# Turning the order of wide and narrow matmuls from chunk to chunk in the weight-stationary projections

## The chip, the cores and the metric

The kernel runs on one core of a Trainium2 chip; the other cores are idle. The metric is the device time of one execution in microseconds (us), the median of a few runs. The engines of the core are named as in the profile: PE is TensorE (its matmuls), PEld its weight loads, DVE is VectorE, ACT is ScalarE, POOL is GpSimd and SP is SyncE, whose queue issues the DMAs.

## The reference

A small decoder trunk of two layers over 256 positions and 1024 channels, in float32. Every sub-layer is applied as a post-norm with a scaled residual. The gated feed-forward network (FFN) stands twice in each layer and has an inner width of 2816:

```python
def swiglu(x, w_gate, w_up, w_down):
    return (jax.nn.silu(x @ w_gate) * (x @ w_up)) @ w_down

for l in range(DEPTH):                                   # DEPTH = 2
    x = layer_norm(alpha * x + 0.5 * swiglu(x, gate[l, 0], up[l, 0], down[l, 0]), ...)
    mem_kv = mem @ w_kv_mem[l]                           # 256 memory tokens
    u = x @ w_in_conv[0]  or  x @ w_in_mlstm[0]          # layer 0, layer 1
    tok = short_conv_mixer(u[...])  or  mlstm_mixer(u[...])
    xa = memory_cross_attention(u[..., -256:], mem_kv)
    x = layer_norm(alpha * x + concat([tok, xa]) @ w_out[l], ...)
    x = layer_norm(alpha * x + 0.5 * swiglu(x, gate[l, 1], up[l, 1], down[l, 1]), ...)
```

The output is the last x, 256 by 1024.

## The kernel before

Float32 matmuls are made of float32r products. Each operand is split into a high part, rounded to float32r, and a low part, the rest. The product of two operands is then high times high, high times low and low times high. Weights arrive by DMA on the SP queue in pieces of 128 x 2048 (`raw`). `split` (lines 98 to 100) turns each piece into a high tile `wh` (a copy on ACT, line 99) and a low tile `wl` (a subtraction on DVE, line 100), mostly in halves of 1024 columns. Five pieces can be held split at a time and three raw ones. The order of the pieces is a list written out at the start; the next piece is loaded and split when an earlier one is taken with `get`.

Activations are kept transposed in tiles of `[128, 8, 2, 256]`: eight chunks `k` of 128 channels, and in each the high and the low part of 256 positions side by side, 512 columns in all.

There are two ways of multiplying:

- **`mm3` (lines 171 to 177)**: the activation is the stationary operand, the weights stream past it. For each chunk it issues three matmuls, 512 columns wide mostly. The down projection of the FFN (`y`), the output projection (`yo`) and the first groups of the later FFNs (`gx`) are made like this.
- **`mmw` (lines 179 to 182)**: the weights are the stationary operand ("weight-stationary"). For each chunk it issues a pair: a wide matmul with `wh` that streams all 512 columns (high and low positions), and a narrow one with `wl` that streams the 256 columns of the high part into the first half of the same PSUM bank. Eight chunks are summed in one bank; then `comb` (lines 184 to 187) adds the two halves, on ACT (line 186) and DVE (line 187). Each matmul here has a weight load of its own, 128 x 128.

`mmw` is called from `gu_ws` (lines 271 to 303), the gate and up projection of one group of 256 inner channels: four banks of eight chunks each, 32 pairs; from `mem_kv` (line 388, tiles `kb`); and from `proj_ws` (line 407), which serves the cross-attention's query (`xq`), the gates and the input of the convolution (`cg`, `cx`, `cb`) and the query and key of the mLSTM (`qkp`).

An FFN runs over 11 groups `g`. A steady step is one `gu_ws` (32 pairs) and one `down` of the group before (24 matmuls of `mm3`, 512 wide). In the first FFN all groups go through `gu_ws`, and for `g` below 2 the loop over chunks is the outer one and the four banks the inner one; in the three other FFNs the groups 0 and 1 go through `gu_xs` (tiles `gx`) and the remaining nine through `gu_ws`.

The program is written in the Tile framework, which finds the waits between engines itself and may put instructions of an engine in another order than the source where it expects an operand later than another. So in group 2 of the first FFN some wide matmuls stand ahead of their narrow ones.

Of the kernel before, what the change touches and what calls it, by code (L numbers as in the profile page):

```python
# [14 lines left out]
P = 128  # L15
T = 256
D = 1024
KC = D // P
# [13 lines left out]
def trunk(ctx: ExitStack, tc: tile.TileContext, d, out):  # L32
    nc = tc.nc
    pe, act, dve, pool = nc.tensor, nc.scalar, nc.vector, nc.gpsimd
# [16 lines left out]
    def mbank(name):  # L51
        return psm.tile([P, 512], F32, tag="mm", name=name)

    def tmp(name):
        return tp.tile([P, 512], F32, tag="t", name=name)
# [79 lines left out]
    def get(*key):  # L135
        while state["next"] < len(pieces) and state["next"] <= state["used"] + 1:
            trace_piece()
        assert pieces[state["used"]][0] == key, (pieces[state["used"]][0], key)
        state["used"] += 1
        return made.pop(key)  # L140
# [11 lines left out]
    for k in range(KC):  # L152
# [3 lines left out]
        s = slice((k % 4) * 512, (k % 4) * 512 + 512)  # L156
# [3 lines left out]
    cur = {"x": x0}  # L160
# [10 lines left out]
    def mm3(o, a, b, start, stop):  # L171

        ah, al = a
        bh, bl = b
        pe.matmul(o, ah, bh, start=start, stop=False)  # L175
        pe.matmul(o, ah, bl, start=False, stop=False)  # L176
        pe.matmul(o, al, bh, start=False, stop=stop)  # L177

    def mmw(bank, w, a, start, stop):

        pe.matmul(bank, w[0], a.rearrange("p c t -> p (c t)"), start=start, stop=False)  # L181
        pe.matmul(bank[:, :T], w[1], a[:, 0], start=False, stop=stop)  # L182

    def comb(o, bank):

        act.activation(o, bank[:, T:], AF.Copy)  # L186
        dve.tensor_add(o, o, bank[:, :T])  # L187
# [4 lines left out]
    def xpart(k, t):  # L192
        return cur["x"][:, k, 0, tsl(t)], cur["x"][:, k, 1, tsl(t)]
# [70 lines left out]
    def ffn(l, j, xs_groups, i, last=False):  # L264
        hT = {}
        y = {}

        def new_h(g):
            hT[g] = hp.tile([P, 2, 2, T], F32R, tag="h", name=f"h{l}{j}_{g}")

        def gu_ws(g, outer=False):
            w = [get("gu", l, j, g, 0), get("gu", l, j, g, 1)]
            new_h(g)
            banks = {}

            def mm(fc, m, k):
                if k == 0:
                    bank = ybank if outer and g == 0 else mbank
                    banks[fc, m] = bank(f"gu{l}{j}_{g}_{fc}{m}")
                c0 = (k % 4) * 512 + m * 256 + fc * P  # L280
                wk = w[k // 4]
                mmw(banks[fc, m], (wk[0][:, c0:c0 + P], wk[1][:, c0:c0 + P]), cur["x"][:, k],
                    k == 0, k == KC - 1)

            if outer:
                for k in range(KC):
                    for fc in range(2):
                        for m in range(2):
                            mm(fc, m, k)
            for fc in range(2):  # L290
                t_ = tmp(f"s{l}{j}_{g}_{fc}")
                for m in range(2):
                    if not outer:
                        for k in range(KC):
                            mm(fc, m, k)
                    comb(t_[:, m * 256:(m + 1) * 256], banks[fc, m])
                    if m == 0:
                        act.activation(t_[:, :256], t_[:, :256], AF.Silu)  # L298
                dve.scalar_tensor_tensor(t_[:, 256:], t_[:, :256], 0.5, t_[:, 256:],  # L299
                                         op0=ALU.mult, op1=ALU.mult)  # L300
                hh = hT[g][:, 0, fc, :]
                act.activation(hh, t_[:, 256:], AF.Copy)  # L302
                dve.tensor_sub(hT[g][:, 1, fc, :], t_[:, 256:], hh.bitcast(F32))  # L303

        xsw = {}

        def gu_xs(g, t, mid=None):
            if t == 0:
                xsw[g] = [get("gu", l, j, g, 0), get("gu", l, j, g, 1)]
                new_h(g)  # L310
            w = xsw[g]
            b = mbank(f"gx{l}{j}_{g}_{t}")
            for k in range(KC):
                wk = w[k // 4]
                s = slice((k % 4) * 512, (k % 4) * 512 + 512)
                mm3(b, xpart(k, t), (wk[0][:, s], wk[1][:, s]), k == 0, k == KC - 1)
                if k == 5 and mid:
                    mid()
            t_ = tmp(f"sx{l}{j}_{g}_{t}")
            act.activation(t_[:, :256], b[:, :256], AF.Silu)  # L320
            dve.scalar_tensor_tensor(t_[:, 256:], t_[:, :256], 0.5, b[:, 256:],
                                     op0=ALU.mult, op1=ALU.mult)

            def rest():
                hx(g, t, t_)
            return rest

        def hx(g, t, t_):
            tb = mbank(f"hx{l}{j}_{g}_{t}")
            for fc in range(2):  # L330
                pe.transpose(tb[:, fc * P:(fc + 1) * P], t_[:, 256 + fc * P:256 + (fc + 1) * P], ident)
            tv = tb[:, :256].rearrange("p (c t) -> p c t", c=2)
            hh = hT[g][:, 0, :, tsl(t)]
            act.activation(hh, tv, AF.Copy)
            dve.tensor_sub(hT[g][:, 1, :, tsl(t)], tv, hh.bitcast(F32))

        def down(g, t, hs, w):
            for fc in range(2):
                a = (hT[g][:, 0, fc, tsl(t)], hT[g][:, 1, fc, tsl(t)])
                for h in hs:  # L340
                    if (t, h) not in y:
                        y[t, h] = ybank(f"y{l}{j}_{t}{h}")
                    s = slice(fc * D + 512 * h, fc * D + 512 * h + 512)
                    mm3(y[t, h], a, (w[0][:, s], w[1][:, s]), g == 0 and fc == 0,
                        g == NG - 1 and fc == 1)

        late = []
        for t in range(2):
            for g in range(xs_groups):
                late.append(gu_xs(g, t, pending if (t, g) == (0, xs_groups - 1) else None))  # L350
                if len(late) > 1:
                    late.pop(0)()
        for g in range(NG):
            if g == 2:
                if i == 0:
                    late_loads()
                gb = load_ln(i)
            if g >= xs_groups:
                gu_ws(g, outer=(l, j) == (0, 0) and g < 2)
                while late:  # L360
                    late.pop(0)()
            for q in downs_after(g, xs_groups):
                w = get("wd", l, j, q)
                for t in range(2):
                    down(q, t, (0, 1), w)
        nx = None if last else new_act(f"x{i}")
        ws = {g: get("wd", l, j, g) for g in range(NG - TAIL, NG)}

        def tail(t):
            for h in range(2):  # L370
                for g in range(NG - TAIL, NG):
                    down(g, t, (h,), ws[g])
                ln_half(i, t, h, y[t, h])
        norm_both(i, gb, nx, tail)
# [4 lines left out]
    def mem_kv(mem):  # L379
        w = [get("kv", q) for q in range(4)]  # L380
        for l in range(2):
            kvs[l] = (consts.tile([P, 2, T], F32, name=f"kT{l}"), consts.tile([P, 2, T], F32, name=f"vm{l}"))
        for c in range(4):
            b = mbank(f"kb{c}")
            for k in range(KC):
                s = slice((k % 2) * D + c * P, (k % 2) * D + (c + 1) * P)
                wk = w[k // 2]
                mmw(b, (wk[0][:, s], wk[1][:, s]), mem[:, k], k == 0, k == KC - 1)
            comb(kvs[c // 2][0][:, c % 2], b)
        pending()  # L390
        for c in range(2):
            b = mbank(f"vb{c}")
            for k in range(KC):
                s = slice((k % 2) * D + 512, (k % 2) * D + 1024)
                wk = w[k // 2]
                mm3(b, (mem[:, k, 0, tsl(c)], mem[:, k, 1, tsl(c)]), (wk[0][:, s], wk[1][:, s]),
                    k == 0, k == KC - 1)
            for l in range(2):
                act.activation(kvs[l][1][:, c], b[:, l * 256:(l + 1) * 256], AF.Copy)

    def proj_ws(w, name, use):

        for c in range(2):
            b = mbank(f"{name}_{c}")
            for k in range(KC):
                s = slice(k * 256 + c * P, k * 256 + (c + 1) * P)
                mmw(b, (w[0][:, s], w[1][:, s]), cur["x"][:, k], k == 0, k == KC - 1)
            use(c, b)

    def proj_to(o, w, name):  # L410
# [349 lines left out]
    mem = get("mem")  # L760
# [9 lines left out]
    o = OutProj(0, mix, 1)  # L770
# [61 lines left out]
```

## Time and profile before

| what | before |
|---|---|
| median of the runs | 997.99 us (997.73 to 2501.07, three runs) |
| profiled execution | 997.18 us, of which the span from first to last instruction is 995.3 us |
| granted TensorE clock | 0.997 of full speed on the mean |
| PE busy | 981.8 us, 99% of the span, 5116 matmuls |
| weight loads busy | 831.1 us, 83% |
| DVE, ACT busy | 666.3 us (67%), 530.9 us (53%) |
| DMA | 186.90 MB, 188 GB/s on the mean |

The span is the time that the engines' records cover; the execution's own time has 1.9 us more around it. A row of a group reads: line of the kernel, engine, operation, output and inputs by name, shape, number of instructions, then the busy time in us and the mean of one in ns, then the idle time ahead of them and what ended most of it. Busy times of matmuls overlap, since one is begun while another is still draining; how long a matmul holds PE is therefore read from the distance between the starts of two neighbours. In the timeline a row begins with the start in us and the duration in us, and neighbours with the same shape are merged into one row ("x2").

### The profile page before, as it was taken

What the parts mean: (1) busy time and instruction counts of PE and PEld (TensorE: products, weight loads), DVE (VectorE), ACT (ScalarE), POOL (GpSimd) and SP (SyncE); (2) the same over time, 40 slices, a digit from 0 to 9 for tenths busy, and PEclk for the clock granted to TensorE, in tenths of its full rate; (3) what the DMA queues carried; (4) which work ended last, traced back from release to release, by engine and by line L of the source; (5) the groups of instructions that cost most, each with busy time, mean ns of one, the idle gap of its engine ahead of it and who ended that gap; (6) DMA issues with size and microseconds to landing.
All of it is one profiled execution on the core that took longest, in us unless ns stands there. A gap on an engine that the chain in (4) does not pass through costs nothing.

```text
span 995.3 us, 12995 instructions
## 1 busy us (share of the span) xinstructions
PE 981.8 (99%) x5116; PEld 831.1 (83%) x5116; DVE 666.3 (67%) x1024; ACT 530.9 (53%) x851; POOL 28.3 (3%) x38
## 2 busy tenths in 40 slices
PE   9999999999999999999999999999999999999996
PEld 7888888888888888888888888889788788888885
DVE  6686556868677656565865656577588987565555
ACT  7665555457445555555355555435676345455540
POOL 0000000000000000000000000001300100000000
PEclk9999999999999999999999999999999999999999
DMA  8794646465535654645464545434245556546421
GB/s 298 296 317 151 222 156 231 161 233 208 180 130 190 241 203 150 230 143 197 165 258 170 208 173 198 172 112 148 85 159 201 209 217 249 199 145 224 154 85 43
DMA packets 29294, 186.90 MB, mean 188 GB/s; under 512 B 3633, under 2 KB 4657, under 8 KB 8369
## 3 DMA queue, kind: packets, MB, share of 16 engines
q1 hardware_dynamic: 28944, 185.55, 51.8%
q8 instruction: 40, 0.66, 0.2%
q10 hardware_dynamic: 288, 0.52, 0.1%
q14 instruction: 22, 0.17, 0.1%
HBM read 185.01 MB, written 1.05 MB: 187 GB/s over the span
## 4 chain that ended last, share of the span: by engine, by line
PE 94%; DVE 2%; POOL 1%; issue 1%; DMA 0%; ACT 0%; SPq 0%; DVEq 0%; POOLq 0%
PE gu L181 28%; PE gu L182 14%; PE y L175 8%; PE y L177 8%; PE y L176 8%; PE gx L175 2%; PE qkp L181 2%; PE gx L177 2%; PE gx L176 2%; PE cx L181 1%; PE qkp L182 1%; PE cb L181 1%; PE cg L181 1%; PE yo L175 1%; PE yo L177 1%
## 5 line engine op out<-in xcount | busy, mean ns | idle before, releaser
L100 DVE TENSOR_TENSOR wl<-raw,wh 128x1024 fp32r<-128x1024 f32 (+1 forms) x342 | 400.8, 1196 | 149.9 <-ACT wh L99 149.3
L181 PE MATMUL gu<-x,wh 128*128 128x512 f32 x1216 | 430.4, 398 | 0.0
L99 ACT ACTIVATE wh<-raw 128x1024 fp32r<-128x1024 f32 (+1 forms) x342 | 338.5, 1033 | 119.8 <-PE y L177 40.0
L182 PE MATMUL gu<-x,wl 128*128 128x256 f32 x1216 | 340.8, 281 | 0.2 <-DVE wl L100 0.2
L181 PEld LDWEIGHTS gu<-x,wh 128*128 128x128 f32 x1216 | 228.4, 188 | 56.0 <-ACT wh L99 0.3
L182 PEld LDWEIGHTS gu<-x,wl 128*128 128x128 f32 x1216 | 229.6, 189 | 2.2 <-DVE wl L100 0.9
L175 PE MATMUL y<-wh,h 128*128 128x512 f32 x352 | 138.7, 394 | 0.0
L177 PE MATMUL y<-wh,h 128*128 128x512 f32 x352 | 137.3, 391 | 0.0
L176 PE MATMUL y<-wl,h 128*128 128x512 f32 x352 | 136.9, 390 | 0.0
L187 DVE TENSOR_TENSOR s<-s,gu 128x256 f32<-128x256 f32 x152 | 63.2, 418 | 105.7 <-ACT s L186 105.5
L186 ACT ACTIVATE s<-gu 128x256 f32<-128x256 f32 x152 | 57.5, 380 | 108.4 <-PE gu L182 108.0
L175 PEld LDWEIGHTS y<-wh,h 128*128 128x128 f32 x352 | 66.0, 188 | 15.0 <-ACT h L302 1.1
L177 PEld LDWEIGHTS y<-wh,h 128*128 128x128 f32 x352 | 66.0, 188 | 14.7 <-DVE h L303 0.2
L176 PEld LDWEIGHTS y<-wl,h 128*128 128x128 f32 x352 | 66.2, 188 | 12.8
L302 ACT ACTIVATE h<-s 128x256 fp32r<-128x256 f32 x76 | 31.8, 418 | 66.1 <-DVE s L299 66.0
L298 ACT ACTIVATE s<-s 128x256 f32<-128x256 f32 x76 | 31.7, 417 | 37.5 <-DVE s L187 37.5
L303 DVE TENSOR_TENSOR h<-s,h 128x256 fp32r<-128x256 f32 x76 | 32.1, 422 | 17.6 <-ACT h L302 17.5
L175 PE MATMUL gx<-wh,x 128*128 128x512 f32 x96 | 38.2, 398 | 0.0
L176 PE MATMUL gx<-wl,x 128*128 128x512 f32 x96 | 37.4, 390 | 0.0
L177 PE MATMUL gx<-wh,x 128*128 128x512 f32 x96 | 37.3, 391 | 0.0
L181 PE MATMUL qkp<-x,wh 128*128 128x512 f32 x96 | 35.8, 412 | 0.0
L299 DVE SCALAR_TENSOR_TENSOR s<-s 128x256 f32<-128x256 f32 x76 | 32.0, 422 | 1.4
(191 smaller groups left out, 961.5 us busy)
## 6 DMA issues: line engine op xcount, KB each, us to landing
raw<-in_wgu SPq DMA_DIRECT2D x83, 1024.0 KB, 4.8
raw<-in_wd SPq DMA_DIRECT2D x43, 1024.0 KB, 4.8
raw<-in_wconv SPq DMA_DIRECT2D x10, 1024.0 KB, 4.8
raw<-in_wout SPq DMA_DIRECT2D x8, 1024.0 KB, 4.7
raw<-in_wm SPq DMA_DIRECT2D x7, 1024.0 KB, 4.9
gb<-in_lngb SPq DMA_DIRECT2D x6, 1024.0 KB, 4.7
raw<-in_wkv SPq DMA_DIRECT2D x4, 1024.0 KB, 4.8
raw<-in_wop SPq DMA_DIRECT2D x4, 776.0 KB, 4.2
```

The lines of the kernel that those rows point to most:

```text
L99: act.activation(h, raw, AF.Copy)
L100: dve.tensor_sub(l, raw, h.bitcast(F32))
L175: pe.matmul(o, ah, bh, start=start, stop=False)
L176: pe.matmul(o, ah, bl, start=False, stop=False)
L177: pe.matmul(o, al, bh, start=False, stop=stop)
L181: pe.matmul(bank, w[0], a.rearrange("p c t -> p (c t)"), start=start, stop=False)
L182: pe.matmul(bank[:, :T], w[1], a[:, 0], start=False, stop=stop)
L186: act.activation(o, bank[:, T:], AF.Copy)
L187: dve.tensor_add(o, o, bank[:, :T])
L299: dve.scalar_tensor_tensor(t_[:, 256:], t_[:, :256], 0.5, t_[:, 256:], op0=ALU.mult, op1=ALU.mult)
L302: act.activation(hh, t_[:, 256:], AF.Copy)
L303: dve.tensor_sub(hT[g][:, 1, fc, :], t_[:, 256:], hh.bitcast(F32))
```

## The change

`mmw` gets the chunk's number `k` instead of the two flags. In even chunks it issues the wide matmul and then the narrow one, as before; in odd chunks the narrow one and then the wide one. Over the chunks the order is wide, narrow, narrow, wide, wide, narrow, narrow, wide and so on. The first matmul of a bank is still the wide one of chunk 0, which clears the bank; the last is now the wide one of chunk 7. The number of matmuls, their operands and their shapes stay as they are.

```diff
-    def mmw(bank, w, a, start, stop):
-
-        pe.matmul(bank, w[0], a.rearrange("p c t -> p (c t)"), start=start, stop=False)
-        pe.matmul(bank[:, :T], w[1], a[:, 0], start=False, stop=stop)
+    def mmw(bank, w, a, k):
+
+        for part in ((0, 1), (1, 0))[k % 2]:
+            o, b = (bank[:, :T], a[:, 0]) if part else (bank, a.rearrange("p c t -> p (c t)"))
+            pe.matmul(o, w[part], b, start=(k, part) == (0, 0), stop=(k, part) == (KC - 1, 0))
...
-                mmw(banks[fc, m], (wk[0][:, c0:c0 + P], wk[1][:, c0:c0 + P]), cur["x"][:, k],
-                    k == 0, k == KC - 1)
+                mmw(banks[fc, m], (wk[0][:, c0:c0 + P], wk[1][:, c0:c0 + P]), cur["x"][:, k], k)
...
-                mmw(b, (wk[0][:, s], wk[1][:, s]), mem[:, k], k == 0, k == KC - 1)
+                mmw(b, (wk[0][:, s], wk[1][:, s]), mem[:, k], k)
...
-                mmw(b, (w[0][:, s], w[1][:, s]), cur["x"][:, k], k == 0, k == KC - 1)
+                mmw(b, (w[0][:, s], w[1][:, s]), cur["x"][:, k], k)
```

In the program that is built, PE's order at the start of a steady group (group 3 of the first FFN, first bank; `gu_3_00` is the bank, `x` the activations, `wh` and `wl` the split weights of a piece) was:

```order
L181 MATMUL gu_3_00_578<-x_110,wh_529 128x512 [waits DVE_49,Activation_49]
L182 MATMUL gu_3_00_578<-x_110,wl_530 128x256 [waits DVE_49]
L181 MATMUL gu_3_00_578<-x_110,wh_529 128x512
L182 MATMUL gu_3_00_578<-x_110,wl_530 128x256
L181 MATMUL gu_3_00_578<-x_110,wh_529 128x512 [waits Activation_49]
L182 MATMUL gu_3_00_578<-x_110,wl_530 128x256 [waits DVE_49]
L181 MATMUL gu_3_00_578<-x_110,wh_529 128x512
L182 MATMUL gu_3_00_578<-x_110,wl_530 128x256
```

At the same place it is now (both matmuls are issued from line 183):

```order
L183 MATMUL gu_3_00_578<-x_110,wh_529 128x512 [waits DVE_49,Activation_49]
L183 MATMUL gu_3_00_578<-x_110,wl_530 128x256 [waits DVE_49]
L183 MATMUL gu_3_00_578<-x_110,wl_530 128x256
L183 MATMUL gu_3_00_578<-x_110,wh_529 128x512
L183 MATMUL gu_3_00_578<-x_110,wh_529 128x512 [waits Activation_49]
L183 MATMUL gu_3_00_578<-x_110,wl_530 128x256 [waits DVE_49]
L183 MATMUL gu_3_00_578<-x_110,wl_530 128x256
L183 MATMUL gu_3_00_578<-x_110,wh_529 128x512
```

The pair of every second chunk is turned; the waits on the split weights stay at the even chunks, where a new half of a piece begins.

On DVE the order is the same but for a few casts of weights in the convolution's and the mLSTM's stage. Around the first `cx` projection (tiles `ct`), where `wl_2284` is the low part of the piece after it, DVE had:

```order
L187 TENSOR_TENSOR ct_2055<-ct_2055,cx_0_2064 128x256
L100 TENSOR_TENSOR wl_2284<-raw_2282,wh_2283 128x1024
L187 TENSOR_TENSOR ct_2055<-ct_2055,cx_1_2083 128x256
L100 TENSOR_TENSOR wl_2284<-raw_2282,wh_2283 128x1024
L516 TENSOR_TENSOR ct_2055<-cgs_1956,ct_2055 128x512
```

and now has:

```order
L188 TENSOR_TENSOR ct_2055<-ct_2055,cx_0_2064 128x256
L188 TENSOR_TENSOR ct_2055<-ct_2055,cx_1_2083 128x256
L516 TENSOR_TENSOR ct_2055<-cgs_1956,ct_2055 128x512
L100 TENSOR_TENSOR wl_2284<-raw_2282,wh_2283 128x1024 x2
```

The casts went behind the second half of the projection and the product with the gate.

## The prediction

> **What bounds the kernel now.** I read the profile page first, then the chain of waits on it, then the groups, and then the timeline of PE alone, since the starts of neighbouring matmuls tell what each one costs.
>
> ```profile
> PE 981.8 (99%) x5116; PEld 831.1 (83%) x5116; DVE 666.3 (67%) x1024; ACT 530.9 (53%) x851; POOL 28.3 (3%) x38
> ...
> PE 94%; DVE 2%; POOL 1%; issue 1%; DMA 0%; ACT 0%; SPq 0%; DVEq 0%; POOLq 0%
> PE gu L181 28%; PE gu L182 14%; PE y L175 8%; PE y L177 8%; PE y L176 8%; PE gx L175 2%; PE qkp L181 2%; PE gx L177 2%; PE gx L176 2%; PE cx L181 1%; PE qkp L182 1%; PE cb L181 1%; PE cg L181 1%; PE yo L175 1%; PE yo L177 1%
> ...
> L100 DVE TENSOR_TENSOR wl<-raw,wh 128x1024 fp32r<-128x1024 f32 (+1 forms) x342 | 400.8, 1196 | 149.9 <-ACT wh L99 149.3
> L181 PE MATMUL gu<-x,wh 128*128 128x512 f32 x1216 | 430.4, 398 | 0.0
> ...
> L182 PE MATMUL gu<-x,wl 128*128 128x256 f32 x1216 | 340.8, 281 | 0.2 <-DVE wl L100 0.2
> ...
> L182 PEld LDWEIGHTS gu<-x,wl 128*128 128x128 f32 x1216 | 229.6, 189 | 2.2 <-DVE wl L100 0.9
> ```
>
> The reader is to see that PE carries the end: it is 94% of the chain, and the gate and up pairs, the change's own instructions, are 28% and 14% of it. PE hardly waits there (0.2 us ahead of 1216 narrow matmuls). So only a change in the spacing of matmuls can move the time. The durations of 398 and 281 ns overlap and are no price. The price is in the starts. The next rows are from PE's timeline over one steady step of the first FFN: 32 pairs, then 24 matmuls of the down projection.
>
> ```profile
> 51.15 0.39 PE L181 MATMUL gu<-x,wh 128*128 128x512 f32 x1
> ...
> 62.09 0.40 PE L181 MATMUL gu<-x,wh 128*128 128x512 f32 x1
> 62.33 0.28 PE L182 MATMUL gu<-x,wl 128*128 128x256 f32 x1
> 62.44 0.40 PE L175 MATMUL y<-wh,h 128*128 128x512 f32 x1
> 62.68 0.40 PE L176 MATMUL y<-wl,h 128*128 128x512 f32 x1
> 62.92 0.40 PE L177 MATMUL y<-wh,h 128*128 128x512 f32 x1
> ...
> 65.23 0.39 PE L175 MATMUL y<-wh,h 128*128 128x512 f32 x1
> ...
> 67.72 0.39 PE L177 MATMUL y<-wh,h 128*128 128x512 f32 x1
> 67.95 0.39 PE L181 MATMUL gu<-x,wh 128*128 128x512 f32 x1
> ```
>
> The 32 pairs last from 51.15 to 62.44: 11.29 us, 352.8 ns each; the last one has 0.24 us from wide to narrow (62.09 to 62.33) and 0.11 on to the next wide. The down projection's wide matmuls begin at 240 ns (62.44, 62.68, 62.92) and settle: the 11 from 65.23 to 67.72 take 226.4 each. All 24 take 5.51 us, where 24 at 226.4 would be 5.43.
>
> The same pairs run faster elsewhere in this trace. The last four pieces of the mLSTM's query and key have:
>
> ```profile
> 738.16 0.39 PE L181 MATMUL qkp<-x,wh 128*128 128x512 f32 x1
> ...
> 755.14 0.39 PE L181 MATMUL qkp<-x,wh 128*128 128x512 f32 x1
> ```
>
> There are 49 pairs between these two starts: 16.98 us, 346.5 ns each. So one and the same order has two spacings, 352.8 and 346.5, and the slow one loses 6.3 ns a pair. I take 346.5 for the floor: 226.4 for a wide one leaves 120 for a narrow one.
>
> **The change part by part.** It adds and removes no instruction. What is new is a narrow after a narrow and a wide after a wide. The trace has both, since group 2 of the first FFN was built in another order than its source:
>
> ```profile
> 39.40 1.11 PE L181 MATMUL gu<-x,wh 128*128 128x512 f32 x4
> 40.34 0.27 PE L182 MATMUL gu<-x,wl 128*128 128x256 f32 x1
> ...
> 40.69 0.40 PE L182 MATMUL gu<-x,wl 128*128 128x256 f32 x2
> 40.93 0.39 PE L181 MATMUL gu<-x,wh 128*128 128x512 f32 x1
> ...
> 42.20 0.40 PE L182 MATMUL gu<-x,wl 128*128 128x256 f32 x2
> 42.43 0.40 PE L181 MATMUL gu<-x,wh 128*128 128x512 f32 x1
> ...
> 45.67 0.39 PE L175 MATMUL y<-wh,h 128*128 128x512 f32 x1
> 45.90 0.40 PE L176 MATMUL y<-wl,h 128*128 128x512 f32 x1
> ```
>
> *Narrow after narrow.* Two in a row take 0.24 us (40.69 to 40.93) and 0.23 us (42.20 to 42.43), 115 to 120 ns each. That is no more than a narrow costs before a wide one. The second one's weight load is therefore hidden under the first.
>
> *Wide after wide.* The four at 39.40 take 0.94 us, 235 each; in the slow spacing the first ones after a narrow take 240 (62.44); after the fast stretch the first takes 0.23 (45.67 to 45.90). The ends are 226 and 240.
>
> *What the turned rows do to the rest.* From 40.93 to 45.67 there are 13 wide and 15 narrow ones in 4.74 us. At 226.4 and 120 they would take 4.74; at the slow spacing, 6.3 ns more for each narrow one, 4.84. After the first two narrow neighbours the stretch is at the floor to its end, although most of its pairs stand in the old order. This is the nearest row to the changed order, so I take the fast spacing for the changed pairs. The other end is no gain.
>
> The sum, against the profiled execution's 997.2 us:
> - Steady groups: eight of the first FFN (groups 3 to 10) and nine in each of three others, 35 groups of 32 pairs, 1120 pairs at 6.3 ns: -7.1 us. From no change: 0.
> - The down projection behind each: 5.51 us after a slow group, 5.48 (45.67 to 51.15) after the faster one; 0.03 x 35 = -1.0 us.
> - The 304 pairs outside the FFNs (by the loops: 32 of `kb`, 32 of `xq`, 144 of the convolution, 96 of `qkp`): between 0 and 304 x 6.3 ns = -1.9 us. Some are fast already, as shown; I take -0.8.
> - Waits: in a steady group the waits on `wl` stand at even chunks, where the wide one still leads, so nothing is new. Where each chunk has a cast of its own (first group of the first FFN, first bank of `kb`), the narrow one of an odd chunk now waits for `wl` without a wide one running ahead of it: at most one wide, 0.23 us, in 4 + 4 odd chunks, 1.8 us. It counts only where PE waits for casts at all, which is 0.9 us by the PEld row above. I take +0.5.
> - The few casts that moved back on DVE, in the convolution and the mLSTM: the waits for `wl` are all in these rows of its tile:
>
> ```profile
> who waited for it (us, times):
>   PEld gu L182: 0.9, 2
>   PEld sc L431: 0.2, 1
>   PEld kb L182: 0.2, 1
>   PE gu L182: 0.2, 1
> ```
>
> No `cx`, `cb` or `qkp` row waits for one, so the pieces cast ahead cover the move: 0. Uncovered, one cast of 1196 ns late is 1.2 us at a place.
> - The end of a bank: ACT and DVE now follow a wide matmul instead of a narrow one; the next bank's matmuls run meanwhile: 0.
>
> The sum is 997.2 - 7.1 - 1.0 - 0.8 + 0.5 = 988.8 us. The median of the runs lies 0.8 above the profiled execution, so the forecast is 989.6.
>
> One thing can shift any kernel here: after a gap in the mLSTM's gates PE runs at a lower clock for a few us.
>
> ```profile
> 719.00:723.00 4.00, 4.00 (x14) 3.44 (x15) 3.25 (x8) 3.74 (x9) 0.00 (x0) 0.57 0.00 0
> ```
>
> ```profile
> 719.36 0.62 PE L181 MATMUL qkp<-x,wh 128*128 128x512 f32 x1
> ...
> 722.55 0.50 PE L181 MATMUL qkp<-x,wh 128*128 128x512 f32 x1
> ```
>
> In the first row, from a table of stretches, the granted clock is the third number from the end, 0.57; in the timeline's rows five pairs take 3.19 us instead of 1.73. It is there before and after; lost or doubled it is 1.5 us either way, which goes into the range.
>
> **The rivals.**
>
> *Order does not matter.* Each matmul has its price by its width, and the slow spacing belongs to the mix of widths, however they are ordered: the time stays 998.0. For it: the slow spacing holds in every steady group, and down projections, which are all wide, do not carry the fast state into the next group (51.15 begins a slow one). Against: the same order at 346.5, and the stretch after 40.93. The Trainium skill ("TensorE: Matmul & The Clock Gate", section "Back-to-back issue gap") gives a gap from the width alone, N/2.4 + 2.5 ns, so an order could neither gain nor lose; its estimate for a pair is 325 ns. The trace's pairs lie 9% and 7% above that, and differ from each other at the same widths, which the rule doesn't have.
>
> *Wide after wide keeps its 240 ns.* If each wide one that follows a narrow one and precedes a wide one stays at 240, two turned pairs cost 240 (wide to narrow) + 120 + 115 + 240 = 715, against 2 x 352.8 = 705.6: +9.4 ns for two pairs, 560 times in the steady groups, +5.3 us: 1003. For it: the 0.94 us at 39.40 and the 240s at 62.44. Against: 45.67 to 45.90. It decides from the point where the second wide starts over 233 ns after the first.
>
> *The second narrow waits for its load*, the slow side. A load is 189 ns long in the PEld row and a narrow's stream 120; if the load of the second is not begun under the first, narrow after narrow costs 189 at least, 69 ns more, in 760 places: +52 us, 1050. It would need a narrow-to-narrow distance over about 150 ns. Against: both rows of two narrows, at 115 to 120.
>
> **How the numbers follow.** Forecast 0.50; order does not matter 0.27; wide after wide at 240 0.14; late load 0.04; the rest, 0.05, lies between the first two but for 0.02 on something better than any row here. The range, 987 to 1002, reaches from the forecast with every pair outside the FFNs fast and no new waits, 988, less 1 for the clock's stretch, up to 1002, which holds the first rival with its own clock shift and waits, and that part of the second in which the wide ones stand at 238 rather than 240. What is left out is the rest of the second, the late load and the 0.02 below: under 2 in 10. About 2% (20 us) is what a measurement of this kernel can tell from no change; below 978 I see 0.02, above 1018 the late load's 0.04, and 0.94 between.
>
> **What would show it.** Right: a steady step of 16.80 us (51.15 to 67.95) becomes about 16.57 (32 x 346.5 ns and 5.48 us); two narrows take 0.23 to 0.24 us and a wide follows a wide at 0.23. The first rival: the step stays at 16.80. The second: wides at 0.24 after a wide and a step near 16.95. The third: two narrows take over 0.3 us. The forecast is wrong also if rows of `wl` appear among PE's waits in `kb` or the convolution with more than 2 us.

## The result, and the profile after

The changed kernel takes 991.36 us (median of six runs) against 999.29 us of the kernel before, run beside it. The ratio is 0.9926, with a 95% interval of 0.991 to 0.9942: 7 us faster, a small gain and a clear one. One of the six runs took 1069.55 us at a granted clock of 0.85; the ratio is of the others. The forecast was 989.6 against a median of 997.99, so -8.4 us; the range of 987 to 1002 holds the time. The profiled execution took 990.83 us, with a span of 989.0 (995.3 before).

The page of the changed kernel, cut to what answers to the lines shown of before:

```profile
PE 975.6 (99%) x5116; PEld 828.6 (84%) x5116; DVE 666.4 (67%) x1024; ACT 529.6 (54%) x851; POOL 28.3 (3%) x38
...
PE 92%; DVE 2%; POOL 1%; issue 1%; DMA 1%; ACT 0%; SPq 0%; DVEq 0%; POOLq 0%
PE gu L183 42%; PE y L175 8%; PE y L177 8%; PE y L176 8%; PE qkp L183 3%; PE gx L175 2%; PE gx L176 2%; PE gx L177 2%; PE cx L183 2%; PE cg L183 2%; PE cb L183 2%; PE kb L183 1%; PE yo L175 1%; PE yo L177 1%; PE yo L176 1%
...
L183 PE MATMUL gu<-x,wh 128*128 128x512 f32 x1216 | 390.2, 396 | 0.0
...
L183 PE MATMUL gu<-x,wl 128*128 128x256 f32 x1216 | 243.6, 279 | 0.1
```

PE is still the chain. The mean durations of a wide and a narrow matmul, 396 and 279 ns, are 2 ns less than before (398 and 281): durations show next to nothing of the gain, as they overlap. The starts show it. From PE's timeline of one steady step (start in us, duration in us; neighbours of one shape are merged):

```profile
52.10 0.39 PE L183 MATMUL gu<-x,wh 128*128 128x512 f32 x1
52.32 0.40 PE L183 MATMUL gu<-x,wl 128*128 128x256 f32 x2
52.56 0.63 PE L183 MATMUL gu<-x,wh 128*128 128x512 f32 x2
53.03 0.39 PE L183 MATMUL gu<-x,wl 128*128 128x256 f32 x2
53.25 0.63 PE L183 MATMUL gu<-x,wh 128*128 128x512 f32 x2
...
62.31 0.63 PE L183 MATMUL gu<-x,wh 128*128 128x512 f32 x2
...
63.24 0.39 PE L175 MATMUL y<-wh,h 128*128 128x512 f32 x1
63.47 0.39 PE L176 MATMUL y<-wl,h 128*128 128x512 f32 x1
...
68.68 0.39 PE L183 MATMUL gu<-x,wh 128*128 128x512 f32 x1
```

The 32 pairs now take 11.14 us (52.10 to 63.24) where they took 11.29, 348.2 ns a pair in place of 352.8. The 24 matmuls of the down projection take 5.44 us (63.24 to 68.68) where they took 5.51: their first ones are no longer 240 ns apart (63.24 to 63.47). A step is 16.58 us where it was 16.80. Added up from start to start over the two traces, the matmuls of the 35 steady groups take 5.2 us less and the down projections 1.6 less, a little more than the 6.3 us by which the span is shorter; about 1 us of it went in the first two groups of the first FFN. There the first down projection begins at 30.02 us, and began at 29.02 before:

```profile
5.84 0.63 PE L183 MATMUL gu<-x,wh 128*128 128x512 f32 x1
6.27 0.41 PE L183 MATMUL gu<-x,wl 128*128 128x256 f32 x1
...
30.02 0.40 PE L175 MATMUL y<-wh,h 128*128 128x512 f32 x1
```

The first matmuls have the durations of a lowered clock here (0.63 and 0.41, as the pairs after 719 us before), and before they had 0.46 and less: the first three pairs take 1.92 us (5.84 to 7.76) where they took 1.11. That it was the clock is read from these durations alone, since the record of the granted clock sets in only at 8.28 us here. This microsecond is not the same in every execution: four later kernels with the same order in these two groups (runs of three, four and eight, and two by two) began their first down projection between 29.13 and 30.23.

### The profile page after: what moved, and what is told of

Its sections match the earlier page's. It is cut to its first block, busy times and chain, and to the rows that moved or that the text cites. A ratio compares the mean times of both kernels' runs of the same rounds, so it can differ in the third digit from the quotient of the medians.

```text
span 989.0 us, 12985 instructions
## 1 busy us (share of the span) xinstructions
PE 975.6 (99%) x5116; PEld 828.6 (84%) x5116; DVE 666.4 (67%) x1024; ACT 529.6 (54%) x851; POOL 28.3 (3%) x38
## 4 chain that ended last, share of the span: by engine, by line
PE 92%; DVE 2%; POOL 1%; issue 1%; DMA 1%; ACT 0%; SPq 0%; DVEq 0%; POOLq 0%
PE gu L183 42%; PE y L175 8%; PE y L177 8%; PE y L176 8%; PE qkp L183 3%; PE gx L175 2%; PE gx L176 2%; PE gx L177 2%; PE cx L183 2%; PE cg L183 2%; PE cb L183 2%; PE kb L183 1%; PE yo L175 1%; PE yo L177 1%; PE yo L176 1%
## 5 line engine op out<-in xcount | busy, mean ns | idle before, releaser
L183 PE MATMUL gu<-x,wh 128*128 128x512 f32 x1216 | 390.2, 396 | 0.0
L183 PE MATMUL gu<-x,wl 128*128 128x256 f32 x1216 | 243.6, 279 | 0.1
L183 PEld LDWEIGHTS gu<-x,wh 128*128 128x128 f32 x1216 | 190.1, 189 | 3.5
L261 ACT ACTIVATE x<-xt 128x512 fp32r<-128x512 f32 x20 | 11.3, 597 | 40.6 <-PE xt L240 40.3
```

The source lines that it names most:

```text
L183: pe.matmul(o, w[part], b, start=(k, part) == (0, 0), stop=(k, part) == (KC - 1, 0))
```

## The experiments

What was to be found out is why an order should matter at all. The forecast rested on two readings of the trace: that two narrow matmuls in a row cost nothing extra, and that after such a place PE stays in a faster spacing. Each experiment below is read by the **gate-up part** of a steady step (from the first wide matmul of a group to the first of the down projection) and the **step** (to the next group), from the starts in PE's timeline; these repeat to 0.01 us over the steady steps of a run. The rows are rounded to 0.01 us, so that a difference of two of them can be off by as much from the table. The floor, from the wide matmuls' 226.7 ns and 120 ns for a narrow, is 32 x 346.7 = 11.09 us for the part.

| kernel | gate-up part | ns a pair | down part | median time, ratio to before |
|---|---|---|---|---|
| before (one, one) | 11.29 | 352.8 | 5.51 | |
| turned (two, two) | 11.14 | 348.2 | 5.44 | 991.36; 0.9926 (0.991 to 0.9942) |
| one chunk turned | 11.27 | 352.2 | 5.45 | 995.59; 0.9973 (0.9959 to 0.9987) |
| two, two, not turned | 11.14 | 348.0 | 5.45 | 990.33; 0.9926 (0.9911 to 0.9941) |
| runs of three | 11.18 | 349.3 | 5.45 | 993.68; 0.9968 (0.9955 to 0.9981) |
| runs of four | 11.22 | 350.5 | 5.47 | 992.63; 0.9938 (0.9916 to 0.996) |
| runs of eight | 11.15 | 348.3 | 5.47 | 992.96; 0.9947 (0.9927 to 0.9966) |

### One chunk turned

```diff
-        for part in ((0, 1), (1, 0))[k % 2]:
+        for part in ((0, 1), (1, 0))[k == 1]:
...
-            pe.matmul(o, w[part], b, start=(k, part) == (0, 0), stop=(k, part) == (KC - 1, 0))
+            pe.matmul(o, w[part], b, start=(k, part) == (0, 0), stop=(k, part) == (KC - 1, 1))
```

> Only chunk 1 of each bank is turned: one pair of narrow neighbours and one of wide neighbours in eight chunks, three quarters of the narrow matmuls stand alone between two wide ones as before. Theory 'lone narrow' (each narrow that stands alone between two wide ones costs some ns over its stream, a pair of narrows hardly): a quarter of the gain, a steady step of about 16.75 us (16.80 before, 16.59 with every second chunk turned), time about 996 us. Rival 'state' (one place with two narrows puts PE into the fast spacing, and it stays there till the next down projection, as after 40.93 us in the profile of before): nearly the whole gain, a step of 16.60 us, time about 991 us.

From PE's timeline of this kernel, the first matmul of a group, of its down projection and of the next group:

```profile
101.36 0.39 PE L183 MATMUL gu<-x,wh 128*128 128x512 f32 x1
...
112.63 0.40 PE L175 MATMUL y<-wh,h 128*128 128x512 f32 x1
...
118.08 0.39 PE L183 MATMUL gu<-x,wh 128*128 128x512 f32 x1
```

The part is 11.27 us, the step 16.72. One turned place in eight chunks brings 0.02 us of the 0.15: a turned place leaves no lasting fast spacing behind it. The reading on which the forecast leaned, that the stretch after 40.93 us was fast because of the narrow neighbours in it, is not borne out. (It is not tried in just that form: here the two narrows are followed by two wides, there by a single one.) A quarter of the gain was expected by the other theory and an eighth came in the pairs; the down part got nearly all of its own, so the time, 995.6, is close to the 996 of that theory.

### Runs of four and of eight

The wide and the narrow matmuls of a bank are issued from a list of (chunk, part):

```diff
+    SEQ = [(0, 0), (1, 0), (1, 1), (0, 1), (2, 1), (3, 1), (3, 0), (2, 0),
+           (4, 0), (5, 0), (5, 1), (4, 1), (6, 1), (7, 1), (7, 0), (6, 0)]     # runs of four
+    SEQ = [(k, 0) for k in range(KC)] + [(k, 1) for k in range(KC)]             # runs of eight
...
+        for n, (k, part) in enumerate(SEQ):
+            ...
+            pe.matmul(o, ws(k)[part], b, start=n == 0, stop=n == 2 * KC - 1)
```

> Within a bank the matmuls go in runs of four of one width (two wide, four narrow, four wide, four narrow, two wide; the next bank begins with two wide). 'Lone narrow' or 'change of width' (the loss belongs to the places where the width changes): half as many changes as in the turned kernel, a step of about 16.56 us, time about 990 us. Rival 'supply with a short buffer' (matmul and load come at about 177 ns each on average, and only a few are held ahead; a run of four narrows at 120 ns needs 227 ns of lead): a step above the turned kernel's 16.59 us, between 16.6 and 16.9, time 992 to 1002 us.

> Each bank does its eight wide matmuls and then its eight narrow ones. 'Change of width': two changes in sixteen matmuls, nothing left to lose, a step of 16.53 to 16.55 us (the floor is 32 x 346.7 + 24 x 226.7 ns = 16.53), time about 989 us, less or more what later casts of the low parts change at the start of a stage. 'Supply with a short buffer': eight narrows need 453 ns of lead; what is not held ahead is lost at every bank, a step of 16.7 us or more, time 995 or more.

Neither theory fits both kernels. The runs of four came out as the supply theory had it (a step of 16.69 us, a time of 992.6), the runs of eight (16.61) as neither had. Fewer changes of width are not better: runs of four are worse (11.22) than runs of two (11.14), and runs of eight no better (11.15). The time of the eights, 993.0, is above the turned kernel's, too, but the two intervals overlap, and of the 2.5 us between the two spans 2.2 lie in the output projection of the mLSTM's layer and the transposes behind it (`yo`, `xt`), whose order was not changed; so it is the steady steps that are compared here. The eights show in their timeline how the loss is made, since each run is one row:

```profile
85.07 1.98 PE L191 MATMUL gu<-x,wh 128*128 128x512 f32 x8
86.89 1.12 PE L191 MATMUL gu<-x,wl 128*128 128x256 f32 x8
87.84 2.00 PE L191 MATMUL gu<-x,wh 128*128 128x512 f32 x8
89.68 1.12 PE L191 MATMUL gu<-x,wl 128*128 128x256 f32 x8
90.63 2.00 PE L191 MATMUL gu<-x,wh 128*128 128x512 f32 x8
...
96.22 0.40 PE L175 MATMUL y<-wh,h 128*128 128x512 f32 x1
```

The first eight wides come after the down projection's wides and take 1.82 us (85.07 to 86.89), 8 x 226.7 ns. The next eights come after narrows and take 1.84 us each. The eight narrows take 0.95 us, a little under 8 x 120. So after a change from narrow to wide some 27 ns are lost and after one from wide to narrow some 7 come back. In nanoseconds, as the mean of the steady steps, the wides after a narrow start 233, 236, 228, 232 and 231 ns apart and then 227, the narrows 113, 119 and then 120. This suggests that a long run pays the price once and that a short one ends before all of it is paid; that reading fits the sums and was not tried by itself.

### Two by two, not turned, and runs of three

```diff
+    SEQ = [(k + q, part) for k in range(0, KC, 2) for part in range(2) for q in range(2)]    # two, two
+    SEQ = [(0, 0), (1, 0), (2, 0), (0, 1), (1, 1), (2, 1), (3, 0), (4, 0), (5, 0), (3, 1), (4, 1), (5, 1),
+           (6, 0), (7, 0), (6, 1), (7, 1)]                                                   # three, three
```

> Runs of two as in the turned kernel, but in the order wide 0, wide 1, narrow 0, narrow 1, wide 2 and so on, so neither two narrows in a row nor a narrow and the wide after it share a chunk in the way they do when turned. Theory 'run length' (only the sequence of widths counts): the same as turned, gate-up part of a step 11.14 us (16.59 for the step), time about 991 us. Rival 'shared operand' (the turned order gains because the narrow and the wide that follow each other read the same activation chunk): back to 11.29 and 998 us.

> Runs of three of one width, and of two at the end of a bank. By 'run length' as the runs so far show it: after a narrow the wide matmuls lose about 6, 10, 1, 6 and 4 ns, in this order, and a run of narrows gives back 7 to 12; runs of two lose 3 ns net, of four 17, of eight 20. A run of three loses 17 and gives back 9: 8 net, so about 5 or 6 runs in two banks: gate-up part 11.14 to 11.18 us, time 991 to 993 us. It would beat the turned kernel only below 11.13.

The first starts its gate-up part at 102.08 and its down part at 113.21, the second at 101.15 and 112.33:

```profile
102.08 0.62 PE L191 MATMUL gu<-x,wh 128*128 128x512 f32 x2
...
113.21 0.40 PE L175 MATMUL y<-wh,h 128*128 128x512 f32 x1
```

```profile
101.15 0.84 PE L192 MATMUL gu<-x,wh 128*128 128x512 f32 x3
...
112.33 0.40 PE L175 MATMUL y<-wh,h 128*128 128x512 f32 x1
```

Two by two without turning gives the turned kernel's step and its ratio to the fourth digit. So it isn't the chunk that neighbours share; of the two theories, the one in which the sequence of widths alone counts holds. Runs of three lie between two and four, as the sum from the run lengths had it (11.14 to 11.18). Their time, 993.7, is above that of the fours and of the 991 to 993 expected; 2.1 us of what their profile takes over the turned kernel's lie in `yo` and `xt`, as with the eights. By the steady step two is the best length of those tried; the times of two, four and eight can't be told apart.

### A wider and a narrower narrow matmul

```diff
-        pe.matmul(bank[:, :T], w[1], a[:, 0], start=False, stop=stop)
+        pe.matmul(bank[:, :320], w[1], a.rearrange("p c t -> p (c t)")[:, :320], start=False, stop=stop)   # 320
+        n = T if stop else 224                                                                             # 224
+        pe.matmul(bank[:, :n], w[1], a[:, 0, :n], start=False, stop=stop)
```

> The order of before, the narrow matmul widened from 256 to 320 columns (it adds the small product of two low parts for 64 positions). Theory 'load' (the load of the wide one's weights needs a little more than the 120 ns that a narrow of 256 columns leaves; runs so far: halving that load took the pair from 352.8 to about 341 ns): a narrow of 320 columns covers the load, the loss of the alternating order is gone, and 64 columns at 0.417 ns add 26.7 ns to the floor pair of 346.7 less what the load held it at: 367 to 373 ns a pair, gate-up part of a step 11.74 to 11.95 us, the down part 5.44. Rival 'alternation' (each change of width costs some ns whatever the load): 352.8 + 26.7 = 379.5 ns a pair, gate-up part 12.14 us.

> The turned order with the narrow matmul at 320 columns. 'Load': with the load covered the order no longer matters, the gate-up part equals that of the old order at 320 columns within 0.02 us. 'Alternation': it stays 0.15 us below it, as at 256 columns (11.29 against 11.14).

> The order of before, the narrow matmul cut from 256 to 224 columns but for the last chunk (32 positions lack their low-weight product there). 'Load': the pair is held by the load and not by the stream, so it stays at about 353 ns (347 to 355), gate-up part 11.1 to 11.3 us. 'Alternation' (stream plus a fixed loss): 13.3 ns less a pair, 339.5 ns, gate-up part 10.9 us.

At 320 columns, in the old order and in the turned one:

```profile
89.13 0.39 PE L181 MATMUL gu<-x,wh 128*128 128x512 f32 x1
...
101.27 0.40 PE L175 MATMUL y<-wh,h 128*128 128x512 f32 x1
```

```profile
88.92 0.39 PE L183 MATMUL gu<-x,wh 128*128 128x512 f32 x1
...
100.97 0.39 PE L175 MATMUL y<-wh,h 128*128 128x512 f32 x1
```

The old order takes 12.14 us, 379.4 ns a pair: the 64 columns add their 26.7 ns to 352.8 (at 106.7 ns between the 512 and the 256 columns of the floor, 0.417 ns each) and nothing is won back. A load that a narrow of 256 columns just fails to cover would have been covered here. That theory falls in this form. Turned, the part is 12.05 us, 0.09 less (0.15 at 256 columns): the order goes on mattering at this width, if less.

At 224 columns the part of a steady step is 11.03 us, 344.8 ns a pair, between the two expectations: in the seven of eight pairs that were cut, about 9 ns were saved and not the stream's 13.3. It decides nothing, and the time of that run, 1017 us, is no measure: PE stood idle in the first FFN waiting for DVE's and ACT's results, and its clock fell, as its table of stretches shows (PE busy first, granted clock third from the end):

```profile
35.00:50.00 15.00, 8.02 (x30) 6.51 (x29) 12.10 (x17) 10.60 (x17) 0.00 (x0) 0.66 0.81 314
```

### Half loads

```diff
+        m = P if start else 64
-        pe.matmul(bank, w[0], a.rearrange("p c t -> p (c t)"), start=start, stop=False)
+        pe.matmul(bank[:m], w[0][:, :m], a.rearrange("p c t -> p (c t)"), start=start, stop=False)   # wide
...
+        m = P if stop else 64
+        pe.matmul(bank[:m, :T], w[1][:, :m], a[:, 0], start=False, stop=stop)                        # narrow
```

> The order of before, but from chunk 1 on the wide matmul has only 64 of its 128 stationary columns, so its weight load, which runs beside a narrow matmul, is shorter (half of the outputs' rows lack their wide products from chunk 1 on). Theory 'load' (the slow spacing comes from the wide one's load not being quite ready under 120 ns of a narrow): pairs fall from 353 to 347 ns, a step of about 16.58 us, a span of about 988. If the load has nothing to do with it: pairs stay at 353 ns, a step of 16.80, a span of about 995.

> The order of before; the narrow matmul has 64 of its 128 stationary columns (half of the outputs' rows lack their low-weight product but for the last chunk), so the load that lies under the wide matmul is halved. 'Load under the narrow': nothing changes, pairs stay at 352.8 ns, gate-up part 11.29 us, span about 995. Rival 'sum of loads' (what matters is all loads together, or the number of rows written): the same as with the wide one's load halved, 10.92 us, span about 984.

With the wide one's load halved, the groups of loads and the timeline show:

```profile
L183 PEld LDWEIGHTS gu<-x,wl 128*128 128x128 f32 x1216 | 228.3, 188 | 2.6 <-DVE wl L100 1.3
L182 PEld LDWEIGHTS gu<-x,wh 128*64 128x64 f32 x1064 | 142.7, 134 | 42.5 <-ACT wh L99 0.3
```

```profile
99.71 0.39 PE L182 MATMUL gu<-x,wh 128*128 128x512 f32 x1
...
110.63 0.40 PE L175 MATMUL y<-wh,h 128*128 128x512 f32 x1
```

A load of 64 columns takes 134 ns where one of 128 takes 188. The part falls to 10.92 us, 341.3 ns a pair: the loss of the alternating order is gone, and 5 ns of what I took for the floor with it. With the narrow one's load halved instead (100.72 to 111.84, 11.12 us, 347.5 ns a pair) the loss is nearly gone too:

```profile
100.72 0.39 PE L181 MATMUL gu<-x,wh 128*128 128x512 f32 x1
...
111.84 0.40 PE L175 MATMUL y<-wh,h 128*128 128x512 f32 x1
```

"Load under the narrow" had no change there and "sum of loads" 10.92; it is neither. The stationary columns, or what goes with them, take part in the loss on both sides. Halving them also halves the rows of PSUM that are written, and these runs can't separate the two.

### Other addresses

```diff
-        pe.matmul(bank[:, :T], w[1], a[:, 0], start=False, stop=stop)
+        o, x = (bank[:, :T], a[:, 0]) if stop else (bank[:, T:], a[:, 1])
+        pe.matmul(o, w[1], x, start=False, stop=stop)
```

> The order of before; all narrow matmuls but the last of a bank read the low positions and write the second half of the bank in place of the first (same widths, other addresses; the low weights then multiply the low parts). Theory 'widths' : no difference, gate-up part 11.29 us, span about 995. Rival 'address' (the loss comes from a narrow that begins anew at the columns that the wide one wrote first): the part moves towards 11.1.

```profile
101.66 0.39 PE L181 MATMUL gu<-x,wh 128*128 128x512 f32 x1
...
112.95 0.40 PE L175 MATMUL y<-wh,h 128*128 128x512 f32 x1
```

The part is 11.29 us (101.66 to 112.95), as before: which half of the bank the narrow one writes, and which half of the positions it reads, has no share in the loss.

### Equal widths

```diff
...
+        n = 512 if start else 384
+        pe.matmul(bank[:, :n], w[0], f[:, :n], start=start, stop=False)
+        if stop:
+            pe.matmul(bank, w[1], f, start=False, stop=True)
+        else:
+            pe.matmul(bank[:, :384], w[1], f[:, :384], start=False, stop=False)
```

> The order of before with both matmuls of a pair at 384 columns, but for the first and the last of a bank, which have 512 (the wide ones leave out half of the low positions' product, the narrow ones add a small product). The mean width is that of before, and the loads are as many. Theory 'change of width': no loss, 173.3 ns from start to start within a bank, gate-up part 4 x (2 x 226.7 + 14 x 173.3) ns = 11.52 us. Rival 'mean supply' (a matmul with its load can't come faster than about 176.5 ns on average, which is what 352.8 ns a pair would be): 176.5 ns from start to start, gate-up part 11.70 us.

One bank of it in PE's timeline, from its first matmul (512 columns) on; the next 14 have 384:

```profile
91.09 0.40 PE L183 MATMUL gu<-x,wh 128*128 128x512 f32 x1
91.32 0.34 PE L187 MATMUL gu<-x,wl 128*128 128x384 f32 x1
91.50 0.34 PE L183 MATMUL gu<-x,wh 128*128 128x384 f32 x1
91.68 0.34 PE L187 MATMUL gu<-x,wl 128*128 128x384 f32 x1
91.86 0.33 PE L183 MATMUL gu<-x,wh 128*128 128x384 f32 x1
92.03 0.33 PE L187 MATMUL gu<-x,wl 128*128 128x384 f32 x1
...
93.77 0.39 PE L185 MATMUL gu<-x,wl 128*128 128x512 f32 x1
```

The first four at 384 columns take 0.71 us (91.32 to 92.03), 177.5 ns each; the ten after them 1.74 us, 174. The pairs here have the mean width and the loads of before, alternate between high and low weights as before, and run at their stream's pace once they have settled. So the mean supply of matmuls and loads is not the limit, nor is it the alternation of tiles. What is left is the change of width: the part is 11.63 us, 0.10 to 0.11 over the 11.52 that it would be without (four banks of 2 x 226.7 ns and 14 x 173.4, midway between the wide's 226.7 and the narrow's 120, which is also what the settled ones take), some 26 ns for each of the four banks. It is of the size of the loss in the runs of eight. A bank has two changes, up to 512 at its end and down to 384 after the next one's first matmul, and in most banks the two stand too close to be told apart; the first bank of a group follows the down projection's wides, has only the change from 512 to 384 ahead of it, and loses the same 26 ns.

## Why the prediction was right

**The bound and the lever** held. PE carries the end before and after, and the gain is in the distance between starts, in the rows that the prediction named.

**Narrow after narrow** held: 0.24 us from 52.32 to 52.56 and 0.22 from 53.03 to 53.25 for two, 115 ns each on the mean of the steady steps, as in the two rows of before. The late load, 0.04 of the chance, did not come.

**Wide after wide** lay in the middle between the two ends: 0.47 us for two (52.56 to 53.03), 233 ns each on the mean of the steady steps. The second wide starts 232 or 233 ns after the first, on the very line that the prediction drew for its rival with 240; that rival's price did not come, since two turned pairs take 2 x 348.2 = 696 ns and not 715. The wides cost more than the forecast's 226.4, the narrows less than its 120.

**The fast spacing** was right in part of its size and wrong in reason. The step that failed is "After the first two narrow neighbours the stretch is at the floor to its end", taken as the nearest row for the whole: one turned chunk a bank leaves no such spacing behind, and the turned order does not run at 346.5 ns but at 348.2, a spacing of its own. What the trace of before shows is that the old order has two spacings, each of which lasts for tens of pairs. The steady groups all have the slow one, in which the starts repeat after three pairs (wide 236, 233, 241 ns, narrow 113, 117, 120); the stretch after 40.93 us, the last pieces of `qkp` and some of the convolution have the fast one, 230 and 117 ns in nearly every pair. One and the same projection, `cb`, has the one in its first place and the other in its second:

```profile
234.55 0.39 PE L181 MATMUL cb<-x,wh 128*128 128x512 f32 x1
...
240.10 0.39 PE L181 MATMUL cg<-x,wh 128*128 128x512 f32 x1
...
253.91 0.40 PE L181 MATMUL cb<-x,wh 128*128 128x512 f32 x1
...
259.56 0.40 PE L181 MATMUL cg<-x,wh 128*128 128x512 f32 x1
```

These are 16 pairs in 5.55 us and 16 in 5.65. In the turned kernel the first of them takes 5.57:

```profile
233.71 0.39 PE L183 MATMUL cb<-x,wh 128*128 128x512 f32 x1
...
239.28 0.39 PE L183 MATMUL cg<-x,wh 128*128 128x512 f32 x1
```

So the turned order wins against the slow spacing and loses a little against the fast one, in which the width changes at every matmul too and a pair takes no more than the floor. What puts the old order into the one or the other wasn't tried and stays open. Two narrow neighbours are not needed for the fast one: the convolution's stretch, from 229.70 us on, has none.

**The sum.** It was 2 us too hopeful: from profile to profile -8.4 us were forecast and -6.3 measured (-7.4 by the ratio of the runs). For the steady groups -7.1 us were put down; 0.15 us in 35 groups is -5.2, since 1.5 of the 6.3 ns a pair remain. For the down projections -1.0 were put down; added up over the two traces they take 1.6 us less, 0.06 each where they stand between two groups. For the pairs outside the FFNs -0.8 were put down, and 0.4 came: 0.5 less in the query and the convolution, nothing in `kb`, and nothing in `qkp`, whose last pieces had the fast spacing already. The first two groups, 1.0 us more in the profiled execution, had no term in the sum but for the waits. The waits for low parts, put down at +0.5, hardly moved; the tile's rows after are

```profile
  PEld gu L183: 0.8, 2
  PEld sc L431: 0.2, 1
  PEld kb L183: 0.2, 1
```

against 0.9, 0.2 and 0.2 before. The casts that moved on DVE cost nothing: no row of the convolution waits for one.

**Order does not matter**, at 0.27, was the rival that the order would not decide a pair's time. At the same widths a pair takes 348.0 to 352.8 ns in the steady groups of these runs, by the order alone, so it falls. A rule of the Trainium skill speaks for it ("TensorE: Matmul & The Clock Gate", section "Back-to-back issue gap": N/2.4 + 2.5 ns, from the width alone; the section calls this the gap of a single matmul). These runs lie 23 to 28 ns a pair above the 325 that the prediction worked out from it, and differ from one another by up to 5.

## What to carry to other kernels

Where PE is the bound, read what a matmul costs from the starts of its neighbours in the timeline, not from its duration, and compare the same pair in several places of the trace: two spacings for one pair say that there is something to win. Where matmuls of two widths must alternate and do so at the slow spacing, put them two by two; longer runs were no better here, and a single turned place in eight chunks brings 0.02 us of the 0.15 in the pairs. Where the alternating order already has its fast spacing, there is nothing to win. A stretch of the trace that happens to contain the new order is a rough measure of its price (346.5 ns a pair there, 348.2 here) and none of its reason: undo the change place by place before the reason is believed.

## What the hardware showed that was not expected

The same matmuls in the same order can settle into two spacings, 346.5 and 353 ns a pair, and stay in either for tens of pairs; the order two by two shows only one in these traces, 348. In the runs of eight a change from 256 to 512 columns has a price that is spread over the next five matmuls, 27 ns in all, of which about 7 come back on the first narrow ones; a change from 512 to 384 costs some 26, spread over the next six. This price is not fixed by the widths, since the fast spacing pays nothing. Run lengths of one, two, three, four and eight cost 6.1, 1.5, 2.6, 3.8 and 1.6 ns a pair above the floor in the steady groups, which is not in the order of their lengths. Half as many stationary columns on either side take most of it away. Which part of PE pays it stays open: that the load is not covered, the addresses, and the mean supply are excluded by the runs above as the whole cause, in the forms tried; the number of stationary columns and the rows written were not separated.
